# Which engine waits for the last stores: GpSimd in place of SyncE at the end of a layer norm with GELU

## Chip, cores, metric

One Trainium2 chip, one core. The metric is the device time of an execution in microseconds (us); the profile's span, first to last instruction, is about 1.8 us shorter (318.5 us in the execution that was timed at 320.32). In the trace's lines SPq, POOLq, ACTq, DVEq and PEldq are the sequencers of SyncE, GpSimd, ScalarE, VectorE and TensorE; DRAIN and NOP are names of instructions.

## The reference

```python
x: (8, 1024, 2048) float32; gamma, beta: (2048,); eps = 1e-5
mean, var over the last axis
out = gamma * (x - mean) / sqrt(var + eps) + beta
return 0.5 * out * (1 + tanh(sqrt(2 / pi) * (out + 0.044715 * out ** 3)))
```

## The kernel before

The 8192 rows are worked in 16 blocks of 4 x 128 rows, in five buffers (slots). SyncE issues the loads, VectorE takes the statistics, GpSimd turns them into scale and bias, ScalarE normalizes, VectorE multiplies by gamma, TensorE adds beta, ScalarE applies GELU and issues the stores. Each slot has a semaphore for its stores. The last block is stored row group by row group:

```python
# ScalarE, last block: four stores of 1 MB, all on the semaphore of slot 4
ac.dma_start(out=og[b, :, q:q + 1], in_=xt[:, q:q + 1])._wait_ge(
    s_r, b + q + 1).then_inc(s_store[slot(b)], 16)
...
with tc.tile_critical(no_gpsimd_drain=True):
    with nc.Block(no_gpsimd_drain=True) as block:
        @block.sync
        ...                      # one function for each engine
    # the block ends here with a barrier of all engines
    for b in range(B, B + SLOTS):
        nc.sync.wait_ge(s_store[slot(b)], stored(b))
# the end of tile_critical adds a handshake, the end of the kernel two more barriers
```

In the trace's records the five waits are two semaphore instructions (line 247), which carry two semaphores each, and a branch (COMPARE_BRANCH, line 107) that carries the fifth. Behind them the trace shows a handshake (line 107), in which SyncE raises a semaphore (at 317.273 us), every engine answers on one of its own (317.312 to 317.359), and SyncE checks all answers (317.438 to 317.564); then a barrier of all engines, a clearing of the semaphores by GpSimd (226 ns, at 318.014), and a last barrier (all line 278). GpSimd leads the barriers: it gathers the arrivals (317.729 and 318.352) and releases the others (317.807 and 318.431).

## Time and profile before

| | before |
|---|---|
| time, median of 3 | 320.14 us (320.01 to 320.34) |
| span | 318.5 us |
| last store issued | 310.320 us |
| last data packet of a store ended | 316.572 us |
| last landing (the semaphore is complete) | 317.034 us |
| last landing to end of span | 1.501 us |

A landing is the moment at which the trace records the last of a transfer's semaphore increments. The quantity from there to the end of the span is called "the tail" below; it is a chain of sequencer instructions alone (from 317.1 us on no engine is busy and the DMA share is 0.00), and I took it from the trace's records in nanoseconds, because the profile's views print tenths of a microsecond.

### The profile page before, as it was taken

To read this page: it belongs to the slowest core of one execution; us is meant where nothing else is said; L and a number is where in the kernel's file an instruction comes from. 1 tells how busy PE (TensorE), PEld (TensorE's weight loads), DVE (VectorE), ACT (ScalarE), POOL (GpSimd) and SP (SyncE) were. 2 spreads that over 40 slices of the span, in tenths; PEclk is the share of its full clock that TensorE was granted. 3 is DMA by queue.
4 is the path that set the end of the run, shared out by engine and by line. 5 is a ranking of instruction groups with operands and counts; after the bars stand their busy time and mean duration, and the time that the engine had idled before them with its cause. 6 is when DMAs were issued, how large, how long until landed. Compare 5 with 4: busy or idle time off the path is not lost.

```text
span 318.5 us, 2090 instructions
## 1 busy us (share of the span) xinstructions
PE 244.3 (77%) x520; PEld 57.2 (18%) x520; DVE 247.5 (78%) x386; ACT 251.7 (79%) x132; POOL 110.6 (35%) x201
## 2 busy tenths in 40 slices
PE   2769999999999989687795868958589595886860
PEld 1212222222212112111121112212112121111110
DVE  3499999999999897786968968599686986869810
ACT  2769999999999989698696967969589695995970
POOL 1144444444444444232443333333332433324300
DMA  7999999999999999999999999999999999999995
GB/s 289 438 457 401 394 434 430 444 424 436 432 424 444 417 453 416 440 440 416 457 403 457 420 436 444 411 461 403 453 432 424 449 407 457 424 432 403 453 396 209
DMA packets 6002, 134.26 MB, mean 421 GB/s; under 512 B 704, under 2 KB 752, under 8 KB 752
## 3 DMA queue, kind: packets, MB, share of 16 engines
q1 hardware_dynamic: 3168, 67.11, 49.4%
q10 hardware_dynamic: 2832, 67.13, 49.0%
q14 instruction: 2, 0.02, 0.0%
HBM read 67.13 MB, written 67.11 MB: 421 GB/s over the span
## 4 chain that ended last, share of the span: by engine, by line
DMA 64%; ACT 14%; DVE 10%; POOL 5%; PE 3%; issue 1%; ACTq 0%; DVEq 0%; POOLq 0%; SPq 0%
DMA xt<-in_x_dram 32%; DMA out_dram<-xt 30%; ACT yk L195 9%; DVE sts L149 7%; ACT xt L202 4%; POOL ves L135 3%; DVE zg L158 2%; PE ps L220 2%; DMA rows<-in_gamma_dram 2%; POOL rss L137 2%; POOL nms L139 1%; DVE mvs L155 1%; PE ps L237 1%; ACT g_t L191 1%; ACTq L205 0%
## 5 line engine op out<-in xcount | busy, mean ns | idle before, releaser
L149 DVE BATCH_NORM_STATS2 sts<-xt 128x6 f32<-128x512 f32 x256 | 157.7, 679 | 33.5 <-DMA xt<-in_x_dram 31.9
L195 ACT ACTIVATE yk<-xt,nms,rss 128x2048 bf16<-128x2048 f32 x64 | 133.7, 2090 | 48.9 <-POOL nms L139 42.9
L237 PE MATMUL ps<-zg,ident 128*128 128x512 bf16 x256 | 120.8, 627 | 55.8 <-DVE zg L158 54.7
L233 PE MATMUL ps<-b_hl,ones_b 33*128 33x512 bf16 x256 | 120.6, 624 | 2.2 <-PEq L228 2.2
L202 ACT ACTIVATE xt<-ps 128x2048 f32<-128x2048 f32 x64 | 118.9, 1858 | 1.5 <-PE ps L237 1.5
L135 POOL TENSOR_SCALAR ves<-mvs 128x1 f32<-128x1 f32 x64 | 38.5, 602 | 179.2 <-DVE mvs L155 179.2
L158 DVE TENSOR_TENSOR zg<-yk,g_t 128x2048 bf16<-128x2048 bf16 x64 | 76.5, 1195 | 19.2 <-ACT yk L195 19.2
L237 PEld LDWEIGHTS ps<-zg,ident 128*128 128x128 bf16 x256 | 27.6, 130 | 149.0 <-DVE zg L158 113.7
L233 PEld LDWEIGHTS ps<-b_hl,ones_b 33*128 33x128 bf16 x256 | 27.0, 127 | 92.1 <-issue 88.4
L139 POOL TENSOR_SCALAR nms<-mvs,rss 128x1 f32<-128x1 f32 x64 | 35.7, 558 | 6.3
L137 POOL TENSOR_TENSOR rss<-ves,mhalf 128x1 f32<-128x1 f32 x64 | 35.3, 552 | 5.3
L155 DVE BATCH_NORM_AGGREGATE mvs<-sts 128x2 f32<-128x24 f32 x64 | 16.9, 264 | 2.2
L220 PE MATMUL ps<-rows,ones 1*128 1x512 f32 x8 | 7.2, 1076 | 6.1 <-DMA rows<-in_gamma_dram 6.1
L188 ACT ACTIVATE b_hl<-rows 1x2048 bf16<-1x2048 f32 x1 | 1.9, 1909 | 5.3 <-DMA rows<-in_beta_dram 5.3
L166 DVE TENSOR_TENSOR b_hl<-rows,b_hl 1x2048 bf16<-1x2048 f32 x1 | 2.3, 2280 | 2.8 <-ACT b_hl L189 2.8
L220 PEld LDWEIGHTS ps<-rows,ones 1*128 1x128 f32 x8 | 2.5, 327 | 9.2 <-DMA rows<-in_gamma_dram 6.1
L191 ACT ACTIVATE g_t<-ps 128x2048 bf16<-128x2048 f32 x1 | 1.9, 1877 | 1.9 <-PE ps L220 1.9
L184 ACT ACT_TABLE_LOAD x1 | 1.3, 1283 | 0.9 <-SPq L107 0.9
L189 ACT ACTIVATE b_hl<-rows 1x2048 bf16<-1x2048 f32 x1 | 1.9, 1908 | 0.0
L161 DVE MEMSET b_hl<- 33x1024 uint32 x1 | 0.9, 912 | 1.2 <-SPq L107 1.2
L126 POOL MEMSET ones<- 65x128 f32 x1 | 0.2, 202 | 0.5 <-SPq L107 0.5
L130 POOL TENSOR_SCALAR_AFFINE_SELECT ident<-ident 128x128 bf16<-128x128 bf16 x1 | 0.3, 295 | 0.1
(7 smaller groups left out, 0.9 us busy)
## 6 DMA issues: line engine op xcount, KB each, us to landing
out_dram<-xt ACTq DMA_DIRECT2D x15, 4096.0 KB, 32.6
xt<-in_x_dram SPq DMA_DIRECT2D x14, 4096.0 KB
xt<-in_x_dram SPq DMA_DIRECT2D x8, 1024.0 KB, 8.4
out_dram<-xt ACTq DMA_DIRECT2D x4, 1024.0 KB, 8.6
rows<-in_beta_dram ACTq DMA_DIRECT2D x2, 8.0 KB, 5.9
rows<-in_gamma_dram ACTq DMA_DIRECT2D x1, 8.0 KB, 5.1
```

Source lines behind the costliest of these rows:

```text
L135: po.tensor_scalar(out=ves[:, c], in0=mvs[:, k, 1:2], scalar1=float(eps), scalar2=1.0, op0=ALU.add, op1=ALU.mult)._wait_ge(s_a, k + 1).the ...
L137: po.tensor_tensor(out=rss[:, c], in0=ves[:, c], in1=mhalf, op=ALU.pow)._wait_ge(s_q, 2 * k + 1).then_inc(s_q, 1)
L139: po.tensor_scalar(out=nms[:, c], in0=mvs[:, k, 0:1], scalar1=rss[:, c], scalar2=-1.0, op0=ALU.mult, op1=ALU.mult)._wait_ge(s_q, 2 * k + 2 ...
L149: ins = ve.bn_stats(out=sts[:, q, j, :], in_=xr[:, j, :])
L155: ve.bn_aggr(out=mvs[:, q], in_=sts[:, q])._wait_ge(s_o, count).then_inc(s_a, 1)
L158: ve.tensor_tensor(out=zgs[q % 2], in0=yks[q % 2], in1=g_t, op=ALU.mult)._wait_ge(s_n, count).then_inc(s_z, 1)
L191: ac.activation(out=g_t, in_=pss[0], func=ACT.Identity)._wait_ge(s_tg, 1).then_inc(s_c, 1)
L195: ac.activation(out=yks[t % 2], in_=xts[slot(b)][:, q], func=ACT.Identity, scale=rss[:, q:q + 1], bias=nms[:, q:q + 1])._wait_ge(s_p, t + ...
L202: ins = ac.activation(out=xt[:, q], in_=pss[i % 2], func=ACT.Gelu_apprx_tanh)._wait_ge(s_t, i + 1)
L220: ins = pe.matmul(pss[0][:, cols(j)], lhsT=ones[64:65], rhs=rows[64:65, j * K // nsub:(j + 1) * K // nsub, :d // K], start=True, stop=True)
L233: ins = pe.matmul(ps[:, cols(j)], lhsT=ones_b, rhs=b_hl[:, cols(j)], start=True, stop=False)
L237: ins = pe.matmul(ps[:, cols(j)], lhsT=ident, rhs=zgs[k % 2][:, cols(j)], start=False, stop=True)
```

## The change

The intent is to take the waiting off SyncE. One word changes:

```diff
         for b in range(B, B + SLOTS):
-            nc.sync.wait_ge(s_store[slot(b)], stored(b))
+            nc.gpsimd.wait_ge(s_store[slot(b)], stored(b))
```

## The prediction

> **What bounds the kernel now.** I read the views in this order: the times, the page's slices and its chain, the table of stages over the last microseconds, the waits of SyncE's queue, and the instructions of the three lines that make up the end. The kernel takes 320.14 us (three runs, 320.01 to 320.34); the profiled span is 318.5 us. The page first:
>
> ```profile
> span 318.5 us, 2090 instructions
> DMA  7999999999999999999999999999999999999995
> GB/s 289 438 457 401 394 434 430 444 424 436 432 424 444 417 453 416 440 440 416 457 403 457 420 436 444 411 461 403 453 432 424 449 407 457 424 432 403 453 396 209
> DMA 64%; ACT 14%; DVE 10%; POOL 5%; PE 3%; issue 1%; ACTq 0%; DVEq 0%; POOLq 0%; SPq 0%
> ```
>
> The DMA row is 9 tenths in every slice but the first and the last, and the chain that ended last is 64% transfers: the body is bound by moving 134.26 MB. The sequencers that only wait (SPq, POOLq) have 0% of the chain. So whatever the change does, it does in the last slice, where the DMA digit falls to 5. The table of stages for that part (columns: stretch, its length, busy time and count for PE, PE weight loads, DVE, ACT and POOL, granted clock, DMA share, GB/s):
>
> ```profile
> 305.00:310.70 5.70, 2.73 (x6) 0.43 (x4) 1.22 (x1) 3.81 (x3) 0.00 (x0) 1.00 0.99 412
> 311.10:316.60 5.50, 0.00 (x0) 0.00 (x0) 0.00 (x0) 0.00 (x0) 0.00 (x0) 1.00 0.63 264
> 316.60:317.10 0.50, 0.00 (x0) 0.00 (x0) 0.00 (x0) 0.00 (x0) 0.00 (x0) 1.00 0.00 0
> 317.10:318.60 1.50, 0.00 (x0) 0.00 (x0) 0.00 (x0) 0.00 (x0) 0.00 (x0) 1.00 0.00 0
> ```
>
> There are four acts: compute ends and the last store is issued (until 310.7); the queue of stores drains with no engine busy (5.5 us); the data has left but the semaphore is not up yet (0.5 us); and 1.5 us in which nothing moves at all, neither engine nor DMA. Who waits through the second and third:
>
> ```profile
> SPq L247 <- DMA out_dram<-xt: 5.9, 1, 5.9
> L247 SPq EVENT_SEMAPHORE  x2: 28/28/28, 311.1 to 317.1; - x2
> L205 ACTq DMA_DIRECT2D out_dram<-xt x4: 338/338/339, 298.3 to 310.3; - x4
> DMA to landing us min/median/max: 6.7/8.6/11.4
> ```
>
> SyncE waits once, 5.9 us, for the stores, all issued long before (the last at 310.3). The wait is two instructions that last 28 ns each when they run, and, as the order of the built program shows, a branch that carries the fifth semaphore. What follows them is the tail, where the change can act:
>
> ```profile
> L107 SPq EVENT_SEMAPHORE  x3: 17/28/28, 317.3 to 317.5; - x3
> L107 SPq COMPARE_BRANCH  x1: 33/33/33, 317.1 to 317.1; - x1
> L107 POOLq NOP  x1: 17/17/17, 317.3 to 317.3; - x1
> L107 SPq NOP  x1: 13/13/13, 317.6 to 317.6; - x1
> L278 POOLq EVENT_SEMAPHORE  x4: 17/17/17, 317.7 to 318.4; - x4
> ```
>
> After the stores are in (317.05), SyncE branches (317.1), raises a semaphore that every other engine waits for (317.3), collects an answer from each of them (317.4 to 317.6), and only then joins the closing barriers, which GpSimd leads (317.7 to 318.4).
>
> [...] the last data packet ended at 316.57, the last landing was recorded at 317.034, 0.46 us later. No choice of waiting engine touches it.
>
> **The change part by part.** Nothing is computed differently. The instruction order of the two built programs differs in one place only: the two waits and the waiting branch leave SyncE and stand on GpSimd, after the barrier that ends the block and before the handshake of line 107. No DMA is issued by SyncE after 251 us, and all stores have been issued before the first of these waits is reached, so neither the transfers nor the 5.9 us of waiting can move: zero from there. What changes is what stands between the last landing (317.034) and the closing barrier.
>
> Before, from the trace's records, starts in us: SyncE's second wait 317.051, its branch 317.118, its raise of the common semaphore 317.273, the four others answer 317.312 to 317.319, SyncE drains 317.359, checks the answers 317.438, 317.497 and 317.564, drains 317.638 and 317.697, and GpSimd's barrier gather fires 317.729. From landing to gather: 317.729 - 317.034 = 0.695 us.
>
> After: while the stores drain, SyncE passes line 107 at once (about 311.3), raises the common semaphore, and ACT, DVE and PE answer; SyncE then stands at its last check, the one for GpSimd's answer. GpSimd alone waits for the stores. Once the last has landed the path is:
> - landing to GpSimd's second wait: 17 ns on SyncE; GpSimd followed ACT's arrival in the block barrier by 31 ns from the end of ACT's instruction. Take 25 ns: 317.06.
> - second wait to branch: 67 ns on SyncE, 78 to 79 ns between GpSimd's semaphore instructions. Take 79: 317.14.
> - branch to the next instruction: 155 ns on SyncE; on GpSimd 190 (launch) and 206 (its loop). Take 190: 317.33.
> - GpSimd's answer to SyncE's last check: an end-to-start step across engines is 24 to 31 ns and the answer lasts 17. Take 45: 317.37.
> - SyncE's check, drain, drain, then the gather on GpSimd: 74 + 59 + 32 ns, as now: 317.54. GpSimd's own drain, 81 ns after its answer and some 78 ns before it can gather, is ready at 317.49, before SyncE.
>
> So 317.54 instead of 317.73: about 0.19 us earlier. The same sum by terms: removed are the raise and its round trip through the others and two of three checks (317.273 to 317.564, 0.29 us); added are the hop from GpSimd to SyncE (0.045) and GpSimd's slower steps (8 + 12 + 35 ns); 0.29 - 0.10 = 0.19 us. The barriers that follow (317.73 to 318.5) are led by GpSimd in both kernels and keep their length. Predicted: span 318.35 us, time 320.14 - 0.19 = 319.95 us, 0.06% less.
>
> **The rivals.** First: GpSimd notices a semaphore later or branches slower than SyncE, and the handshake's saving is eaten. For it: its branch-to-next is 190 to 206 against 155 ns[...]. Against it: [...] a wait, a branch and a no-op stay in its sequencer, whose semaphore instructions last the same 17 ns as SyncE's. To eat 0.19 us it would have to be about three times slower than its steps of 79 ns. Then the time would be 320.1 to 320.3.
>
> Second: the wait is bound by the transfers and everything behind it is hidden or fixed, so nothing changes but noise: 320.14. For it: 5.9 of the last 7.4 us are the drain and the receipt; against it: the 1.5 us behind are serial, with no DMA busy, so a step taken out of them must show in one trace, even if three runs whose spread is 0.33 us can't resolve it.
>
> Third: an idle SyncE or a waiting GpSimd disturbs something else, for instance the stores' draining, and shifts the last landing. Nothing in the profile speaks for it: the stores were queued by ACT, and neither engine issues a descriptor in the last 8 us. If it happened it would be some tenths of a microsecond either way. The same size has the ordinary scatter of the last landing: one of the 16 engines alone still moves 8 KB packets of 309 ns each from 315.05 to 316.57, so which engine is last, and by how many packets, can move the end by 0.3 us a packet. That is larger than the effect.
>
> Fourth: the chain behind the wait grows, because GpSimd is also the leader of the barriers and now arrives last. Its gather needs SyncE's arrival, which now follows its own answer by 0.21 us; its own drain fits inside that. I counted it; had I forgotten the hop, the saving would be 0.05 us larger.
>
> **Range and chances.** The centre is 319.95. The mechanism's own uncertainty is small (0 to 0.3 us of saving); the range is made by run-to-run scatter (0.33 us in three runs) and by a step of one or two packets at the end. I take 319.3 to 320.7, 8 times in 10. A change of 2% is 6.4 us, almost the whole of the last act from the final issue on (8.2 us), and the removable part behind the landing is 1.5 us at most, 0.5%. So faster by over 2%: 0.01, slower by over 2%: 0.01, within 2%: 0.98.
>
> **What would show each step right or wrong.** In the changed profile the line of the two waits should read POOLq instead of SPq, one of them at about 311.1 and the other just after the last landing, and the waits should name POOLq with about 5.9 us. Line 107's branch should be on POOLq. Line 107's instructions on ACT, DVE and PE should stand near 311.3 rather than 317.3, and SyncE's own except its last no-op too; if they still stand after the landing, the step that moves the handshake off the path is wrong. From last landing to the end should be about 1.31 us instead of 1.50; if it is 1.5 or more, the first rival holds. The DMA row, the 5.9 us and the last landing's 0.46 us should be the same within a packet or two. A time outside 319.3 to 320.7 would mean that the transfers themselves moved, which nothing in this argument allows.

The sum came to a gather at 317.54 instead of 317.73 us, 0.19 us saved, 319.95 us.

## The result

The first comparison gave 320.19 us median for both kernels, six runs each (changed 319.88 to 321.24, before 320.01 to 320.34). Its ratio is 1.0005, with a 95% interval of 0.999 to 1.0019. A ratio here is the one that the record gives for the fast runs of the two kernels, so it is not the ratio of the medians. By the times, nothing happened.

The trace shows that something did. The page of the changed kernel, and its table of stages at the end (columns: stretch, its length, then busy time and count for PE, PE weight loads, DVE, ACT and POOL, granted clock, DMA share, GB/s):

```profile
span 318.3 us, 2090 instructions
DMA  7999999999999999999999999999999999999994
```

```profile
311.00:316.60 5.60, 0.00 (x0) 0.00 (x0) 0.00 (x0) 0.00 (x0) 0.00 (x0) 1.00 0.58 243
316.60:317.10 0.50, 0.00 (x0) 0.00 (x0) 0.00 (x0) 0.00 (x0) 0.00 (x0) 1.00 0.00 0
```

The body and the drain of the stores are as before: full DMA slices, then some 5.6 us in which only stores move, then 0.5 us with the data gone and the semaphore not yet up (last data packet to last landing 0.46 us in both: 316.572 to 317.034, now 316.595 to 317.055). Now the lines of the end (line 247 is the waits, 107 the handshake, 278 the closing; columns: operation, count, duration in ns as min/median/max, first and last start in us):

```profile
L247 POOLq EVENT_SEMAPHORE  x2: 43/43/43, 310.2 to 317.1; - x2
```

```profile
L107 SPq EVENT_SEMAPHORE  x3: 17/28/28, 310.2 to 310.4; - x3
L107 SPq NOP  x2: 13/13/13, 0.7 to 317.4; - x2
L107 ACTq DRAIN  x1: 8/8/8, 310.2 to 310.2; - x1
L107 DVEq DRAIN  x1: 19/19/19, 310.2 to 310.2; - x1
L107 SPq DRAIN  x1: 7/7/7, 310.2 to 310.2; - x1
L107 PEldq DRAIN  x1: 13/13/13, 310.3 to 310.3; - x1
L107 POOLq COMPARE_BRANCH  x1: 38/38/38, 317.2 to 317.2; - x1
L107 POOLq NOP  x1: 17/17/17, 317.3 to 317.3; - x1
```

```profile
L278 POOLq EVENT_SEMAPHORE  x4: 17/17/17, 317.5 to 318.2; - x4
```

The waits are GpSimd's. SyncE's three handshake instructions, at 317.3 to 317.5 before, are at 310.2 to 310.4, seven microseconds ahead of the last landing; the answers of ACT, DVE and PE (their DRAINs) are there too. Of line 107, only a branch and an answer of GpSimd and a last no-op of SyncE are left behind the landing, and GpSimd's barriers run 317.5 to 318.2 instead of 317.7 to 318.4. SyncE's queue of waits says the same:

```profile
SPq L107 <- POOLq L107: 6.9, 1, 6.9
```

SyncE now waits 6.9 us for GpSimd's answer, where it waited 5.9 us for the stores. (The difference of 1 us is this run's last store, which was issued 0.97 us earlier, at 309.355; the landing did not follow it.)

The records of both tails, start in us and what follows it:

```
before                                     changed
317.034  last landing                      317.055  last landing
317.051  SyncE   2nd wait                  317.079  GpSimd  2nd wait
317.118  SyncE   branch                    317.166  GpSimd  branch
317.273  SyncE   raises the semaphore      317.332  GpSimd  answers
317.312-317.319  four engines answer       317.375  SyncE   last check (no-op)
317.359  SyncE   drain, answers            317.449  SyncE   drain
317.438, 317.497, 317.564  SyncE checks    317.507  SyncE   drain, arrives
317.638, 317.697  SyncE drains, arrives    317.540  GpSimd  gathers
317.729  GpSimd  gathers                   318.346  end
318.535  end
```

The tail is 1.501 us before and 1.291 us now: 0.21 us less. The landings of the two profiled runs differ by 0.02 us, so the spans differ by 0.19 us (318.535 and 318.346). That is 0.06% of the time.

### The profile page after: what moved, and what is told of

Same layout as the page of the kernel before. It is cut to its first block, busy times and chain, and to the rows that moved or that the text cites. A ratio compares the mean times of both kernels' runs of the same rounds, so it can differ in the third digit from the quotient of the medians.

```text
span 318.3 us, 2090 instructions
## 1 busy us (share of the span) xinstructions
PE 244.3 (77%) x520; PEld 57.1 (18%) x520; DVE 247.3 (78%) x386; ACT 251.7 (79%) x132; POOL 110.4 (35%) x201
## 4 chain that ended last, share of the span: by engine, by line
DMA 64%; ACT 14%; DVE 10%; POOL 5%; PE 3%; issue 1%; ACTq 0%; DVEq 0%; POOLq 0%; SPq 0%
DMA out_dram<-xt 31%; DMA xt<-in_x_dram 31%; ACT yk L195 9%; DVE sts L149 7%; ACT xt L202 4%; POOL ves L135 3%; DVE zg L158 2%; PE ps L220 2%; DMA rows<-in_gamma_dram 2%; POOL rss L137 2%; POOL nms L139 1%; DVE mvs L155 1%; PE ps L237 1%; ACT g_t L191 1%; ACTq L205 0%
```

## Experiments

The theory: behind the last landing there is a serial chain of sequencer steps. What GpSimd waits for, SyncE need not wait for, so SyncE's handshake with the other engines runs while the stores drain and is no longer part of the chain. The engine that waits pays with its own steps. Rivals: GpSimd saves because it is the leader of the barriers; the waiting engine makes no difference; the change costs elsewhere what it saves, as the first ratio above 1 might say. All ten runs gave correct results. The tails were read from one profile each. Experiments 1 to 5 were timed once each; their times decide nothing, and only their tails are used.

### 1. ScalarE waits

```diff
-            nc.gpsimd.wait_ge(s_store[slot(b)], stored(b))
+            nc.scalar.wait_ge(s_store[slot(b)], stored(b))
```

> The five waits stand on ScalarE instead of GpSimd. Theory (the saving is that SyncE's handshake is passed before the stores land; any engine but SyncE gives it): last landing to end of span 1.35 us, from 25 ns to notice, 97 and 150 ns for wait and branch as this engine's records show, 38 ns to SyncE, two checks, two drains and the gather (67+74+59+32 ns) and the closing 0.81 us. Rival (GpSimd saves because it is the leader of the barriers, no other engine would): 1.50 us as with SyncE. The time stays within noise of 320.2 either way.

The handshake and the waits in this run:

```profile
L247 ACTq EVENT_SEMAPHORE  x2: 38/38/38, 311.0 to 316.9; - x2
```

```profile
L107 SPq EVENT_SEMAPHORE  x3: 17/28/6042, 311.0 to 311.2; - x3
...
L107 ACTq COMPARE_BRANCH  x1: 38/38/38, 317.0 to 317.0; - x1
L107 ACTq DRAIN  x1: 8/8/8, 317.2 to 317.2; - x1
```

Measured: tail 1.313 us; one run of 320.19 us beside one of 320.03 us of the kernel before. The saving does not need GpSimd: the first rival falls. The second semaphore instruction of SyncE's checks spans 6042 ns: it stands open from 311.2, held by ScalarE's answer, which comes at 317.2. So in these traces a wait for the second of an instruction's two semaphores stands in its duration (6042 ns here, 6676 ns in experiment 2), while the wait for the first did not: in the kernel before, 28 ns are recorded for the instruction behind 5.9 us of waiting.

### 2. TensorE waits

```diff
-            nc.gpsimd.wait_ge(s_store[slot(b)], stored(b))
+            nc.tensor.wait_ge(s_store[slot(b)], stored(b))
```

> The five waits stand on TensorE, whose sequencer steps are the slowest (150 ns from a semaphore instruction to a branch, 134 to 400 ns after a branch). Theory: the handshake is hidden, but the waiting engine's own steps are on the path, so landing to end is 1.45 to 1.72 us: about as long as before or longer. Rival (which engine waits makes no difference beside hiding the handshake): 1.3 us.

```profile
L107 SPq EVENT_SEMAPHORE  x3: 17/28/6676, 310.4 to 317.3; - x3
...
L107 PEldq COMPARE_BRANCH  x1: 169/169/169, 317.0 to 317.0; - x1
L107 PEldq DRAIN  x1: 13/13/13, 317.2 to 317.2; - x1
```

Measured: tail 1.506 us; one run of 320.12 us beside 320.03 us. The handshake is hidden here too (SyncE's checks begin at 310.4), and still nothing is gained over SyncE's 1.501: TensorE's steps are slow, 111 ns from wait to branch and 227 ns from branch to answer, against 87 and 166 on GpSimd (77 and 160 on ScalarE in experiment 1, 67 and 155 on SyncE in the kernel before), and its answer is among the first that SyncE checks, so two checks remain behind it. Of the 0.215 us by which this tail is longer than the changed kernel's, the steps up to the answer make 0.090 (367 ns from the landing against 277) and the place of the answer in SyncE's order 0.125 (168 ns from the answer to SyncE's last check against 43). On ScalarE the two go opposite ways: the steps are 19 ns shorter than GpSimd's, the one check behind its answer costs 41. So the waiting engine does make a difference, by its place in the order of checks more than by its speed, and the second rival falls.

### 3. GpSimd waits, but inside the block

```diff
                     po.sem_inc(s_q, -2 * R)
+                for b in range(B, B + SLOTS):
+                    po.wait_ge(s_store[slot(b)], stored(b))
...
-        for b in range(B, B + SLOTS):
-            nc.gpsimd.wait_ge(s_store[slot(b)], stored(b))
```

> GpSimd waits for the stores, but at the end of its part of the block, before the barrier that closes it, so that the barrier's release and SyncE's handshake both come after the landing again. Theory (what counts is what stands behind the wait, not who waits): landing to end 1.7 us, longer than before's 1.50: 25 ns, 87 and 166 ns for wait and branch, 78 ns gather to release, 41 ns to SyncE, 66 ns to its raise, 0.456 us handshake, 0.81 us closing. Rival (GpSimd as waiter is what saves): 1.29 us. Rival (nothing but noise): 1.5.

```profile
L144 POOLq EVENT_SEMAPHORE  x2: 43/43/43, 306.8 to 316.6; - x2
```

```profile
L107 SPq EVENT_SEMAPHORE  x3: 17/28/28, 317.1 to 317.3; - x3
L107 SPq NOP  x2: 13/13/13, 0.7 to 317.4; - x2
```

Measured: tail 1.728 us, the longest of the kernels without added barriers; one run of 320.15 us beside 320.03 us. The same engine, the same waits, a few instructions earlier, and the tail is 0.44 us longer than the changed kernel's, because the block's barrier and the whole handshake (317.1 to 317.4) are behind the landing again. It is the place of the wait in the chain that counts. By the records, both kernels need 277 ns from the landing over GpSimd's two waits and branch; the block's barrier then adds 0.189 us here (from its gather to SyncE's raise), and the handshake 0.248 us (0.456 from the raise to the closing gather, against 0.208 from GpSimd's answer to that gather in the changed kernel).

### 4. and 5. The branch taken out, on GpSimd and on SyncE

With the last-landing semaphore (slot 4) waited for last, and a semaphore increment behind it, no wait is left over for the branch to carry, and the branch costs no instruction (line 107 of both runs has no COMPARE_BRANCH):

```diff
-        for b in range(B, B + SLOTS):
+        for b in (B + 4, B, B + 1, B + 2, B + 3):
             nc.gpsimd.wait_ge(s_store[slot(b)], stored(b))      # 4: gpsimd, 5: sync
+        nc.gpsimd.sem_inc(s_par[0], 1)                          # 4: gpsimd, 5: sync
```

> GpSimd waits; the wait for the semaphore that lands last is put last and a semaphore increment behind it takes it up, so that no wait is left to hang on the branch and the branch needs no instruction. Theory of the path (branch step of 166 ns is serial behind the landing): landing to end 1.12 us instead of 1.29. Rival (the path is set by other parts, for instance GpSimd's own drain or SyncE's arrival at the gather): 1.25 to 1.3 us.

> As the kernel before (SyncE waits), but with the wait for the last semaphore put last and taken up by a semaphore increment, so that the branch needs no instruction. Theory: the branch step of 155 ns falls away and the handshake stays behind the landing: landing to end 1.35 us, against 1.12 for the same edit on GpSimd, so the move of the wait is worth about 0.2 us here too. Rival (branch and handshake overlap): 1.50 us.

In experiment 4 (line 248 is the increment, which carries the wait for slot 4):

```profile
L248 POOLq EVENT_SEMAPHORE  x1: 43/43/43, 316.9 to 316.9; - x1
```

```profile
L107 SPq EVENT_SEMAPHORE  x3: 17/28/28, 312.1 to 312.3; - x3
...
L107 POOLq NOP  x1: 17/17/17, 317.0 to 317.0; - x1
```

In experiment 5 SyncE's checks are behind the landing, as in the kernel before:

```profile
L248 SPq EVENT_SEMAPHORE  x1: 28/28/28, 317.1 to 317.1; - x1
L107 SPq EVENT_SEMAPHORE  x3: 17/28/28, 317.2 to 317.4; - x3
```

Measured: tail 1.160 us on GpSimd and 1.359 us on SyncE; one run each, of 319.86 us and 320.24 us. The branch was worth 0.13 us on GpSimd (1.291 to 1.160) and 0.14 us on SyncE (1.501 to 1.359), and it adds to the move of the wait, which is worth 0.20 us in this pair as well. My 1.12 for GpSimd was 0.04 us short: 121 ns pass from the increment to the answer, where my sum had left 87 (87 + 166, less 166).

### 6. and 7. Sixteen barriers, ahead of the waits and behind them

To make the same effect large enough for the clock, sixteen barriers of all engines go in, once ahead of GpSimd's waits and once behind them:

```diff
+        for _ in range(16):                    # 6: here
+            nc.all_engine_barrier()
         for b in range(B, B + SLOTS):
             nc.gpsimd.wait_ge(s_store[slot(b)], stored(b))
+        for _ in range(16):                    # 7: here instead
+            nc.all_engine_barrier()
```

> The changed kernel with 16 barriers of all engines between the block and GpSimd's waits. Theory (what is done before the stores land is free): a barrier is about 0.315 us (gather to release 78 ns, 54 ns to the others, 150 ns PE's drain, 33 ns back), 16 are 5.0 us, less than the 6.9 us until the last landing; landing to end stays 1.29 us and the time 320.2 us. Rival (added synchronization costs its own length wherever it is put): 325.2 us.

> The same 16 barriers after GpSimd's waits. Theory: all of them stand behind the last landing and count in full: landing to end 1.29 + 5.0 = 6.3 us, time 325.2 us, ratio 1.016. Rival (the end of the time taken is the last transfer, and synchronization after it isn't in it): 320.2 us.

GpSimd's barrier instructions of 6 (line 247), then of 7 (line 249):

```profile
L247 POOLq EVENT_SEMAPHORE  x32: 17/17/17, 310.5 to 316.5; - x32
```

```profile
L249 POOLq EVENT_SEMAPHORE  x32: 17/17/17, 317.0 to 322.8; - x32
```

Measured, against 320.37 us (319.87 to 320.86, 11 runs) of the kernel before on the same chip:

| | median, us (4 runs) | ratio, 95% interval | tail, us |
|---|---|---|---|
| 6, ahead | 320.57 (320.31 to 320.91) | 1.0004 (0.9988 to 1.0019) | 1.290 |
| 7, behind | 326.05 (325.98 to 326.59) | 1.0183 (1.0167 to 1.02) | 7.399 |

Sixteen rounds of five engines add nothing that these times resolve while the stores drain (the interval leaves room for 0.6 us at most), and cost their full length once the stores are in: the tail of 7 is 6.11 us longer than the changed kernel's, and its median is 6.0 us above the changed kernel's on the same chip (320.03, experiment 8). Whether the barriers of 6 delay the landing a little is open: its profile has the latest landing of all, 317.83 us, and a tail, counted from the landing, cannot show that. The rival that synchronization costs the same wherever it stands falls, and so does the one that the metric ends with the last transfer. The size in 7 was wrong: I expected a tail of 6.3 us and got 7.4. Most barriers took 0.3275 us, not 0.315 (0.2 us in all), and three of the fifteen intervals were longer by 0.10, 0.27 and 0.47 us. The three late ones were at the same places of the sequence in 6 and in 7 (the 7th barrier, the gather three or four later, the 14th) and came each from another engine (ACT, GpSimd, DVE in 7); what made them late I did not test.

### 8., 9. and 10. The times again

The changed kernel, the kernel of experiment 4, and the kernel before against itself, in five rounds each:

> The changed kernel again, in five rounds against the kernel before. Theory: landing to end is 1.29 us within 0.02, while the last landing itself moves by some tenths of a microsecond from run to run, so the ratio is 1.000 with an interval of about 0.001 and doesn't resolve the 0.2 us (0.0006). Rival (the change costs time elsewhere, as the first ratio of 1.0005 might say): the ratio stays above 1 with an interval that leaves 1 out.

> The kernel of the fourth experiment (GpSimd waits, last semaphore last, no branch) in five rounds. Theory: landing to end 1.16 us within 0.02, 0.34 us less than before, so a ratio of 0.9989; the scatter of the last landing leaves an interval of about 0.0012 to each side, so it may or may not leave out 1. Rival (the shorter tail is given back elsewhere, for instance by a later landing): landing to end 1.16 us but the mean landing later by 0.3 us and a ratio of 1.000.

> The kernel before against itself, in five rounds: what a ratio of two equal kernels looks like. Both theories: landing to end 1.50 us within 0.02, last landing anywhere from 316.6 to 317.8 us, ratio 1.000 with an interval of about 0.0012 to each side. If its ratio is off 1 by as much as those of the changed kernel (1.0005 and 0.9991), no sign of the change can be read from the times.

| | median, us | before, same rounds | ratio, 95% interval | tail, us |
|---|---|---|---|---|
| 8, changed kernel | 320.03 (319.74 to 320.33, 6 runs) | 320.37 (11 runs) | 0.9991 (0.9978 to 1.0003) | 1.291 |
| 9, experiment 4's kernel | 319.81 (319.80 to 319.90, 5 runs) | 320.20 (319.93 to 320.84, 9 runs) | 0.9988 (0.9975 to 1.0002) | 1.159 |
| 10, before | 320.28 (320.06 to 320.47, 5 runs) | 320.20 (9 runs) | 1.0002 (0.9988 to 1.0015) | 1.501 |

The tails repeat to the nanosecond or two, though the runs came from three chips (1 to 4, 5 to 8, 9 and 10): 1.291 and 1.291, 1.160 and 1.159, 1.501 and 1.501. The times do not resolve them. The changed kernel came out at 1.0005 once and at 0.9991 once; the kernel against itself has an interval of the same width; every interval holds 1. The kernel of experiment 4 is the fastest that I ran, by 0.34 us of tail, and all five of its timed runs are below all nine of the kernel before, but its interval still touches 1.0002, so I call this likely and not shown.

Where in the run the scatter sits can be read off the same traces. Over the twelve profiles the last landing lies between 316.61 and 317.83 us, a range of 1.2 us, six times the saving. It does not follow the last issue: that lay at 309.36 us in the changed kernel's first profile and at 311.38 us in experiment 5, and the landings were 317.06 and 317.10; over all twelve the correlation is -0.17. That the transfers as a whole set it would fit a DMA row of nines, but no run tests it. Why the landing varies from run to run is not settled here.

## Why the prediction was right

- **Centre and range.** Predicted 319.95 us within 319.3 to 320.7; measured 320.19, then 320.03 in the repeat. The medians are inside. One run of the first six, 321.24 us, is not: I had taken the scatter from three runs (0.33 us) and the landings scatter by 1.2 us. That the medians lie inside says little: the kernel before, at 320.14 us, lies inside too. What was tested is the tail.
- **The sum.** Predicted were a gather at 317.54, a tail of 1.31 us and a saving of 0.19 us; measured were 317.540, 1.291 us and 0.21 us. Two of the terms were off: wait to branch 87 ns instead of 79, branch to answer 166 instead of 190. With the small terms, landing to gather was 485 ns instead of 506. That the gather came at 317.540 to the nanosecond is luck: the landing itself was 21 ns later. The hop to SyncE, 43 ns, was 45 in the sum, and the three closing steps were 74, 58 and 33 ns against 74, 59 and 32.
- **The handshake leaves the path.** Shown by the starts of line 107 (310.2 instead of 317.3) and, with the cause isolated, by experiments 3 and 1: putting it, and the block's barrier with it, back behind the wait costs 0.44 us with the same engine, and another engine saves as well.
- **First rival, GpSimd's slower steps.** They are real (166 against 155 ns, 87 against 67), but small. With TensorE the whole gain is eaten, 0.09 us by its slower steps and 0.125 by the checks behind its answer, so the rival is true, in part, of another engine.
- **Second rival, nothing but noise.** By the times alone it can't be told from the prediction (320.19 us for both kernels). The repeated tails and experiments 6 and 7 speak against it: what stands behind the landing is in the time taken.
- **Third rival, disturbed transfers.** Nothing shows it, and the times exclude it only down to some tenths of a microsecond (experiment 8: 0.9978 to 1.0003). The scatter of the landing is there in the kernel before too.
- **Fourth rival, GpSimd arrives last.** As counted: SyncE arrives at 317.507 and the gather follows after 33 ns, while GpSimd's own drain was over at 317.461.
- **What I expected of the views.** The waits moved to POOLq as said, but no view lists GpSimd's wait for the stores; it shows only through SyncE, which waits for GpSimd. And SyncE's part was at 310.2, not 311.3, since in that run the last store, and so the block's barrier, came earlier.

## What to carry to other kernels

At the end of a kernel ask what still stands behind the last landing, and put every handshake or barrier that doesn't depend on the stores ahead of the wait for them; the engine to give the wait to is, as far as the four that were tried show it, one whose own steps are short (253 ns from wait to answer on GpSimd, 338 on TensorE) and whose answer is checked last (43 ns from GpSimd's answer to SyncE's last check, 168 from TensorE's). Here that is worth 0.2 us of 320, 0.34 with the branch taken out; my estimate from these figures is that it pays only in kernels much shorter than this one. When an effect is below the scatter of the times, read the one stretch of the trace where it must be, repeat that, and enlarge the cause until the clock shows it.
